# A two-layer transformer trunk on one core: norm total behind the row products, a norm root applied after the product, a rearranged end, and parked gates moved to the later head pairs

## The chip, the cores and the metric

The kernel runs on one core of one Trainium2 chip, in one launch. Its time is the device time in microseconds of that core. The kernel before took 2211.37 us, the median of three runs (2207.99 to 2211.55).

TensorE multiplies a stationary 128x128 block (the weight load, PEld) by a moving block of up to 512 columns and adds into PSUM; VectorE (DVE) and ScalarE (ACT) do elementwise work; SyncE (SP) issues most DMAs; ScalarE can issue DMAs too.

## The reference

Two layers work on 256 context and 256 latent tokens of 1024 channels (`SEQ = CTX_LEN = 256`, `D_MODEL = 1024`, `D_FF = 2816`), in float32. The output is the latent stream after a last norm.

```python
def rmsnorm(x, g):
    y = xf * lax.rsqrt(jnp.mean(xf * xf, axis=-1, keepdims=True) + EPS)
    return y * g
def modulate(h, shift, scale):
    return h * (1.0 + scale) + shift
def swiglu(h, wg, wu, wd):
    return (jax.nn.silu(h @ wg) * (h @ wu)) @ wd
def ffn_half(h_stream, m, gain, w):
    h = modulate(rmsnorm(h_stream, gain), m[0], m[1])
    return h_stream + 0.5 * m[2] * swiglu(h, *w)
...
# trunk_layer, latent stream (context likewise, but not in the last layer)
    x = ffn_half(x, ml[0:3], g[0], p['ffn1'])
    h = modulate(rmsnorm(x, g[1]), ml[3], ml[4])
    u, gq, gk, gv, nq, nk, nv, gates = split_in(h @ p['w_in'])
    y_ssm = s5_mixer(...); y_gqa = window_gqa_latent(...); y_na = neighborhood_attn_latent(...)
    m = sigmoid(g_s) * (y_ssm @ w_p_ssm) + sigmoid(g_a) * (y_gqa @ w_p_gqa) + sigmoid(g_n) * (y_na @ w_p_na)
    x = x + ml[5] * (m @ w_out)
    x = ffn_half(x, ml[6:9], g[2], p['ffn2'])
...
    return rmsnorm(x, final_g)
```

The modulations `ml`, `mc` are `silu(c) @ w_ada + b_ada`, nine of 1024 channels for each layer and stream.

## The kernel before

**Layout.** Channels lie on partitions: `X`, `Hh` and `Hl` are 128 x 8 x 512, columns 0 to 255 the context and 256 to 511 the latent tokens (`HALF` = 256). Every large product is done with both factors split into a high and a low part of a faster type, three matmuls for one (`mm3`, L83 to L85). A weight block of 128x1024 comes by DMA on SP (`wload`, L75), ScalarE makes its high part `whi` (L77), VectorE the remainder `wlo` (L79); three blocks are in flight. Product banks come from a pool of three in PSUM. A framework puts the instructions of each engine into one fixed order when the kernel is built, by priority in the order of the code and by its own model of times; `tc.issue_after(ins)` sets the instructions in its block that run on the engine of `ins` behind it.

**Norm.** `norm_sum` squares the eight blocks on ScalarE (L108) and adds them on VectorE (L109). `norm_total` sums over the partitions by a product with ones (L115, result `nps`). `norm_rsqrt` takes the reciprocal root in eleven small VectorE steps (L122 to L133). `norm_spread` makes it a block of 128 equal rows by products with the identity (L139, `nR`). `norm_apply` multiplies, shifts and splits each block into `Hh` and `Hl` (L158 to L160).

**Start** (`ffn_start`, from L266). The first layer's scale and shift come from row blocks of `w_ada` (`ada_rows`, L284): `products` (L305), `row_copy` (L311), transposition by `shift_scale` (L318, tile `pmod`), then three small VectorE operations (L193, L196). On TensorE `in_turn` keeps the order of the code: 18 warm-up products (`keep_warm`, L336), products of blocks 0 and 1, shift and scale, 12 warm-up products, norm total, spread, and then chunks of the first two feed forward steps between further row products. The two first weight blocks wait with their remainders behind the norm's root. DMAs on SP: row blocks 0 and 1, `X`, two weight blocks, row blocks 2 and 3, two weight blocks, and the rest.

**Mixer** (`mixer`). For each of four head pairs: queries of the windowed attention, its attention, keys, values and queries of the neighbourhood attention, its attention (`attend`: scores L821, softmax, transposition, values). The state-space part (`pump`) runs in pieces between. `gate(j)` is a projection of 24 matmuls and a tanh; `fill()` in front of each of the eight attentions computes gates ahead and parks them in DRAM, one each in layer 0 (seven in all, so none in front of the last), two each in layer 1 (eleven, so none in front of the last two). Three more gates stay on the chip, each behind one of the last three scores. After the attentions their memory is released; then come the splits of their results, the gated unit (`linear_unit`, tile `pgl`), the merge (`branch`, tile `pbr`) and the output product (tile `pwo`, L165 adds to `X`).

**Last feed forward** (`ffn` with one stream, layer 1, n = 1). Two weight blocks are loaded, the norm runs, and then both units of step 0 run block by block (`up`, `gate_up`), followed by steps 1 to 21 and two rounds of down products (tile `pd`). Only the 256 latent columns are computed.

**End** (L1167 to L1171). Norm sum, total, root and spread, then eight output operations, each with a DMA, over four buffers.

## Time and profile before

| what | before |
|---|---|
| median of the timed runs | 2211.37 us (2207.99 to 2211.55) |
| the profiled execution | 2205.09 us, its span 2203.3 us |
| TensorE matmul, busy | 2146.9 us, 97% |
| weight load | 1838.6 us, 83% |
| VectorE | 1621.1 us, 74% |
| ScalarE | 922.6 us, 42% |
| granted TensorE clock, mean | 0.98 |
| DMA | 368.64 MB, mean 167 GB/s |

The span is what the hardware profiler saw from the first to the last instruction of one execution. A busy matmul is not one at the peak: matmuls are pipelined and their ends are modelled, so distances between starts say more than durations. The granted clock is 1.00 at 2.4 GHz and 0.50 at 1.2 GHz. The idle time of an engine that isn't the bound costs nothing.

### The profile page before, as it was taken

To read this page: it belongs to the slowest core of one execution; us is meant where nothing else is said; L and a number is where in the kernel's file an instruction comes from. 1 tells how busy PE (TensorE), PEld (TensorE's weight loads), DVE (VectorE), ACT (ScalarE), POOL (GpSimd) and SP (SyncE) were. 2 spreads that over 40 slices of the span, in tenths; PEclk is the share of its full clock that TensorE was granted. 3 is DMA by queue.
4 is the path that set the end of the run, shared out by engine and by line. 5 is a ranking of instruction groups with operands and counts; after the bars stand their busy time and mean duration, and the time that the engine had idled before them with its cause. 6 is when DMAs were issued, how large, how long until landed. Compare 5 with 4: busy or idle time off the path is not lost. (4 is left out here: it accounts for less than half of the span.)

```text
span 2203.3 us, 32637 instructions
## 1 busy us (share of the span) xinstructions
PE 2146.9 (97%) x12354; PEld 1838.6 (83%) x12354; DVE 1621.1 (74%) x3164; ACT 922.6 (42%) x1560; POOL 0.7 (0%) x6
## 2 busy tenths in 40 slices
PE   7999999999998999999999999999999999999997
PEld 5888888977776888988888888888888888898997
DVE  4897887767765987886777698787857866665555
ACT  3322333466666323422222343223236755644443
POOL 0000000000000000000000000000000000000000
PEclk8999999999999999999999999999999999899999
DMA  8535544543432664675655455555546453453554
GB/s 315 175 119 175 197 159 148 192 134 115 149 106 70 214 221 148 203 231 158 199 198 163 133 165 188 168 170 180 172 125 207 157 172 101 153 198 125 173 191 124
DMA packets 134996, 368.64 MB, mean 167 GB/s; under 512 B 30132, under 2 KB 37044, under 8 KB 134840
## 3 DMA queue, kind: packets, MB, share of 16 engines
q1 hardware_dynamic: 134256, 366.44, 51.2%
q8 instruction: 97, 1.59, 0.3%
q14 instruction: 59, 0.48, 0.1%
q10 hardware_dynamic: 584, 0.12, 0.0%
HBM read 337.40 MB, written 29.11 MB: 166 GB/s over the span
## 5 line engine op out<-in xcount | busy, mean ns | idle before, releaser
L77 ACT ACTIVATE whi<-raw 128x1024 fp32r<-128x1024 f32 (+2 forms) x480 | 455.6, 950 | 950.7 <-issue 318.3
L79 DVE TENSOR_TENSOR wlo<-raw,whi 128x1024 fp32r<-128x1024 f32 (+2 forms) x480 | 520.8, 1087 | 275.0 <-ACT whi L77 273.1
L83 PE MATMUL pgu<-Hh,whi 128*128 128x512 f32 (+1 forms) x1360 | 494.4, 365 | 4.1 <-ACT Hh L159 2.7
L84 PE MATMUL pgu<-Hl,whi 128*128 128x512 f32 (+1 forms) x1360 | 494.3, 364 | 0.0
L85 PE MATMUL pgu<-Hh,wlo 128*128 128x512 f32 (+1 forms) x1360 | 493.8, 363 | 0.5 <-DVE wlo L79 0.5
L83 PEld LDWEIGHTS pgu<-Hh,whi 128*128 128x128 f32 x1360 | 257.9, 190 | 45.5 <-ACT Hh L159 4.4
L85 PEld LDWEIGHTS pgu<-Hh,wlo 128*128 128x128 f32 x1360 | 258.5, 190 | 40.7 <-DVE wlo L79 0.9
L84 PEld LDWEIGHTS pgu<-Hl,whi 128*128 128x128 f32 x1360 | 258.6, 190 | 39.7 <-DVE Hl L160 0.6
L83 PE MATMUL pd<-mid,whi 128*128 128x256 f32 (+1 forms) x836 | 281.1, 336 | 0.0
L84 PE MATMUL pd<-mid,whi 128*128 128x256 f32 (+1 forms) x836 | 280.5, 336 | 0.0
L85 PE MATMUL pd<-mid,wlo 128*128 128x256 f32 (+1 forms) x836 | 280.4, 335 | 0.0
L178 DVE SCALAR_TENSOR_TENSOR ajunk<-araw,sb 128x1024 f32<-128x1024 f32 x208 | 256.0, 1231 | 2.7
L83 PE MATMUL pp<-Hh,whi 128*128 128x512 f32 (+1 forms) x672 | 241.5, 359 | 0.8 <-ACT th L969 0.8
L85 PE MATMUL pp<-Hh,wlo 128*128 128x512 f32 (+1 forms) x672 | 240.4, 358 | 0.0
L84 PE MATMUL pp<-Hl,whi 128*128 128x512 f32 (+1 forms) x672 | 240.4, 358 | 0.0
L84 PEld LDWEIGHTS pd<-mid,whi 128*128 128x128 f32 x836 | 157.4, 188 | 17.8
L83 PEld LDWEIGHTS pd<-mid,whi 128*128 128x128 f32 x836 | 157.4, 188 | 17.8
L85 PEld LDWEIGHTS pd<-mid,wlo 128*128 128x128 f32 x836 | 157.3, 188 | 17.8
L83 PEld LDWEIGHTS pp<-Hh,whi 128*128 128x128 f32 x672 | 130.1, 194 | 17.4 <-ACT th L969 1.9
L84 PEld LDWEIGHTS pp<-Hl,whi 128*128 128x128 f32 x672 | 129.9, 193 | 17.1 <-issue 2.3
L85 PEld LDWEIGHTS pp<-Hh,wlo 128*128 128x128 f32 x672 | 129.7, 193 | 15.4 <-DVE wlo L79 0.2
L243 DVE TENSOR_TENSOR gact<-gact,pgu 128x512 f32<-128x512 f32 (+1 forms) x86 | 53.2, 618 | 70.9 <-PE pgu L85 70.6
(295 smaller groups left out, 2866.9 us busy)
## 6 DMA issues: line engine op xcount, KB each, us to landing
raw<-up SPq DMA_DIRECT2D x176, 512.0 KB, 3.9
araw<-ada SPq DMA_DIRECT2D x104, 512.0 KB, 4.1
raw<-win SPq DMA_DIRECT2D x90, 512.0 KB, 3.8
raw<-dn SPq DMA_DIRECT2D x76, 384.0 KB, 3.1
raw<-dn SPq DMA_DIRECT2D x76, 320.0 KB, 3.0
rw<-ada SPq DMA_DIRECT2D x24, 512.0 KB, 4.3
raw<-wout SPq DMA_DIRECT2D x24, 512.0 KB, 4.3
mid<-ada SPq DMA_DIRECT2D x32, 256.0 KB, 5.0
```

Of the source, the lines that this page charges most:

```text
L77: S.activation(hi[:, :n], raw[:, :n], AF.Copy)
L79: anchor[0] = V.tensor_sub(lo[:, :n], raw[:, :n], hi[:, :n].bitcast(F32)).ins
L83: PE.matmul(out, wh, ah, start=first, stop=False)
L84: PE.matmul(out, wh, al, start=False, stop=False)
L85: pe_anchor[0] = PE.matmul(out, wl, ah, start=False, stop=last).ins
L178: V.scalar_tensor_tensor(junk, raw, 1.0, sb[:, s], op0=ALU.mult, op1=ALU.mult, accum_out=mod[:, l, j, s:s + 1])
L243: V.tensor_mul(g[:, :N], g[:, :N], pu[:, :N])
```

## The change

It has four parts.

1. Start: the second row block's DMAs go to ScalarE's queue, the two tables `bada` and `ng` to SP behind `X`. On TensorE: 18 warm-up products, product of block 0, 9 warm-up products, product of block 1, norm total, shift and scale, spread. In all norms, the shift and the subtraction of the root's first guess become one step.
2. Mixer: the slots of `fill()` are 0, 1, 1, 1, 1, 1, 1, 1 in layer 0 and 1, 1, 1, 1, 1, 2, 2, 2 in layer 1. The three gates that stay may start behind the last query projection, behind the ninth-last score and behind the last score.
3. Last feed forward: `scaled` writes `X` times its coefficient, without the root, right behind each output block, and `shift_column` puts the shift into two columns ahead of the latent ones; the products take 258 columns. `gate_up_late` multiplies the product by the root and adds the shift's product. The norm's total runs between the two units of step 0, its spread behind them, in a PSUM bank of its own.
4. End: the last square goes into the total by its own products, without an addition; 4 and 9 idle products stand around the total; ScalarE scales `X` by the gain ahead of the root; three multiplications and DMAs of 3, 3 and 2 blocks write the output.

```diff
-        yi = y.bitcast(I32)
-        V.tensor_scalar(yi, x.bitcast(I32), 1, None, op0=ALU.arith_shift_right)
-        V.tensor_scalar(yi, yi, -1, 0x5F3759DF, op0=ALU.mult, op1=ALU.add)
+        V.tensor_scalar(y.bitcast(I32), x.bitcast(I32), -0.5, 0x5F3759DF, op0=ALU.mult, op1=ALU.add)
...
+    def norm_total_late(s):
+        cs = stream(s)
+        acc = npool.tile([128, HALF], F32, name="nacc", tag="nacc")
+        S.activation(acc, X[:, 0, cs], AF.Square)
+        for k in range(1, KC):
+            sq = npool.tile([128, HALF], F32, name="nsq", tag="nsq")
+            S.activation(sq, X[:, k, cs], AF.Square)
+            if k < KC - 1:
+                V.tensor_add(acc, acc, sq)
+        ps = nbank[0]("nps")
+        for x in (acc, sq):
+            for j in range(2):
+                pe_anchor[0] = PE.matmul(ps[:, j:j + 1], x[:, 128 * j:128 * j + 128], ones, start=x is acc and j == 0,
+                                         stop=x is sq, skip_group_check=True).ins
+        return ps[:, :2]
...
+    def scaled(l, i, k):
+        ca = coef[:, l, i, 0, k, 1:2]
+        S.activation(Hh[:, k, HALF:], X[:, k, HALF:], AF.Identity, scale=ca)
+        V.scalar_tensor_tensor(Hl[:, k, HALF:], X[:, k, HALF:], ca, Hh[:, k, HALF:].bitcast(F32), op0=ALU.mult, op1=ALU.subtract)
+
+    def shift_column(l, i):
+        cs = slice(HALF - 2, HALF)
+        cb = mod[:, l, 24 * i:24 * i + KC, 1:2].to_broadcast([128, KC, 2])
+        S.activation(Hh[:, :, cs], cb, AF.Copy)
+        V.tensor_sub(Hl[:, :, cs], cb, Hh[:, :, cs].bitcast(F32))
...
+    def gate_up_late(tp, mid, pg, pu, root):
+        late = tp.tile([128, 2], F32, name="late", tag="late", bufs=2)
+        g = tp.tile([128, T], F32, name="gact", tag="gact", bufs=2)
+        for j, p in enumerate((pg, pu)):
+            S.copy(late[:, j:j + 1], p[:, 0:1])
+            V.tensor_mul(g[:, HALF * j:HALF * j + HALF], p[:, 2:HALF + 2], root)
+        S.activation(g[:, :HALF], g[:, :HALF], AF.Silu, bias=late[:, 0:1])
+        V.scalar_tensor_tensor(g[:, :HALF], g[:, HALF:], late[:, 1:2], g[:, :HALF], op0=ALU.add, op1=ALU.mult)
+        split(mid[0][:, HALF:], mid[1][:, HALF:], g[:, :HALF])
...
-            blocks = [ada_rows(0), ada_rows(1)]
+            blocks = [ada_rows(0), ada_rows(1, nc.scalar)]
             for k in range(0, KC, 2):
                 nc.sync.dma_start(X[:, k:k + 2], A["xT"][:, k:k + 2])
+            for t, n in ((bada, "bada"), (ng, "ng")):
+                nc.sync.dma_start(t, A[n])
             in_turn(keep_warm, 18)
-            rows = row_copy(in_turn(products, blocks[0:2]))
-            in_turn(shift_scale, 0, rows)
-            in_turn(keep_warm, 12)
+            pr = in_turn(products, blocks[0:1])
+            in_turn(keep_warm, 9)
+            in_turn(products, blocks[1:2], pr, 1)
...
+            rows = row_copy(pr)
             ps = in_turn(norm_total, acc)
             y = norm_rsqrt(ps)
+            in_turn(shift_scale, 0, rows)
...
-                units = [(bank("pgu"), wload(A["up"][l, n, 0, j], 1024)) for j in range(2)]
-                pieces = norm(l, i, 1)
-                next(pieces)
-                with tc.issue_after(sums[0]), tc.issue_after(sums[1]):
-                    early.append(wload(A["up"][l, n, 1, 0], 1024))
-                for _ in pieces:
-                    pass
-                for k in range(KC):
-                    for ps, w in units:
-                        mm_k(ps[:, :HALF], w, k, HALF, T)
-                up(0, *(ps for ps, w in units))
+                acc = norm_sum(1)
+                first = unit(0, 0)
+                with tc.issue_after(pe_anchor[0]):
+                    y = norm_rsqrt(norm_total(acc))
+                second = unit(0, 1)
+                with tc.issue_after(pe_anchor[0]):
+                    spread = norm_spread(y)[:, :HALF]
+                root.append(tp.tile([128, HALF], F32, name="root", tag="root", bufs=1))
+                S.copy(root[0], spread)
+                up(0, first, second)
...
+        slots = [1, 1, 1, 1, 1, 2, 2, 2] if last else [0, 1, 1, 1, 1, 1, 1, 1]
 
         def fill():
-            for j in queue[:2 if last else 1]:
-                queue.remove(j)
+            for _ in range(slots.pop(0)):
+                j = queue.pop(0)
                 nc.sync.dma_start(parked[j, :, :N], gate(j)[:, :N])
...
             Q = na_queries(c)
+            last_query = pe_anchor[0]
             fill()
...
-        for j, behind in ((1, scored[-3]), (2, scored[-2]), (0, scored[-1])):
+        for j, behind in ((1, last_query), (2, scored[-9]), (0, scored[-1])):
...
-        R = norm_spread(norm_rsqrt(norm_total(norm_sum(1))))[:, :HALF]
+        idle(4)
+        with tc.issue_after(pe_anchor[0]):
+            ps = norm_total_late(1)
+        y = norm_rsqrt(ps)
         for k in range(KC):
-            o = tp.tile([128, HALF], F32, name="o", tag="o", bufs=4)
-            V.scalar_tensor_tensor(o, X[:, k, HALF:], fg[:, k:k + 1], R, op0=ALU.mult, op1=ALU.mult)
-            nc.sync.dma_start(A["out"][:, k], o)
+            S.activation(xg[:, k], X[:, k, HALF:], AF.Copy, scale=fg[:, k:k + 1])
+        idle(9)
+        with tc.issue_after(pe_anchor[0]):
+            R = norm_spread(y)[:, :HALF]
+        for a, b in ((0, 3), (3, 6), (6, 8)):
+            V.tensor_mul(o[:, a:b], xg[:, a:b], R.unsqueeze(1).to_broadcast([128, b - a, HALF]))
+            nc.sync.dma_start(A["out"][:, a:b], o[:, a:b])
```

## Rows read from the trace of the kernel before

**Rows 1.** The page's first part: engine, busy us, share of the span, instructions.
```profile
PE 2146.9 (97%) x12354; PEld 1838.6 (83%) x12354; DVE 1621.1 (74%) x3164; ACT 922.6 (42%) x1560; POOL 0.7 (0%) x6
```

**Rows 2.** Stretches (us), product tile `pgu` alone: length, TensorE busy (matmuls), clock, DMA.
```profile
80.00:120.00 40.00, 40.00 (x178) 1.00 0.51 164
2012.00:2052.00 40.00, 40.00 (x336) 1.00 0.60 196
```

**Rows 3.** Timeline of the start: start us, length us, engine, line, operation, [idle before].
```profile
13.94 5.48 DVE L350 TENSOR_TENSOR mid<-mid 128x512 f32<-128x512 f32 x7 [12.75 <-ACT mid L348]
...
18.21 1.86 PE L318 MATMUL pmod<-pick,rows 128*128 128x2 f32 x8 [6.07 <-ACT rows L311]
...
20.49 4.70 PE L336 MATMUL idle<-ident 128*128 128x128 f32 x24 [0.41 <-DVE mod L193]
...
25.04 0.95 PE L115 MATMUL nps<-ones,mid 128*128 128x1 f32 x8
...
26.22 0.17 DVE L124 TENSOR_SCALAR nt<-nt 128x4 int32<-128x4 int32 x1
...
28.09 2.36 DVE L79 TENSOR_TENSOR wlo<-raw,whi 128x1024 fp32r<-128x1024 f32 x2
...
31.84 1.22 PE L83 MATMUL pgu<-Hh,whi 128*128 128x512 f32 x2 [1.54 <-ACT Hh L159]
```

**Rows 4.** Stretches: length, PE, PEld, DVE, ACT, POOL busy (count), clock, DMA share, GB/s.
```profile
0.00:5.00 5.00, 3.65 (x17) 3.65 (x18) 0.35 (x3) 1.11 (x1) 0.70 (x6) 1.00 0.56 182
...
14.10:24.20 10.10, 5.57 (x25) 5.51 (x26) 5.08 (x10) 7.59 (x11) 0.00 (x0) 0.50 1.04 408
24.30:27.60 3.30, 1.69 (x16) 1.60 (x15) 1.31 (x8) 0.00 (x0) 0.00 (x0) 1.00 1.00 381
27.70:37.80 10.10, 8.04 (x28) 5.87 (x32) 8.19 (x15) 3.71 (x6) 0.00 (x0) 0.50 0.81 288
```

**Rows 5.** Stretches around the last attention of layer 0.
```profile
680.70:693.20 12.50, 6.91 (x20) 4.16 (x18) 7.22 (x18) 9.63 (x18) 0.00 (x0) 0.59 0.12 35
693.30:703.60 10.30, 10.25 (x63) 6.84 (x63) 5.27 (x14) 5.64 (x14) 0.00 (x0) 1.00 0.01 2
703.60:716.40 12.80, 12.80 (x57) 10.59 (x58) 10.21 (x14) 10.58 (x18) 0.00 (x0) 1.00 0.62 221
```

**Rows 6.** Timeline of TensorE there: the first scores.
```profile
683.93 0.80 PE L821 MATMUL sc<-K,Q 128*128 128x256 f32 x2 [2.90 <-DVE Q L753]
```

**Rows 7.** Stretches up to and around the last attention of layer 1.
```profile
1780.00:1870.00 90.00, 88.58 (x568) 74.43 (x568) 67.25 (x146) 56.03 (x116) 0.00 (x0) 0.95 0.46 146
...
1879.00:1886.50 7.50, 3.82 (x8) 1.91 (x8) 5.52 (x12) 5.89 (x13) 0.00 (x0) 0.50 0.33 62
1886.50:1891.20 4.70, 4.70 (x23) 4.69 (x22) 3.07 (x8) 4.31 (x8) 0.00 (x0) 0.50 0.00 0
1891.40:1905.90 14.50, 13.34 (x107) 11.70 (x105) 6.66 (x14) 8.57 (x19) 0.00 (x0) 1.00 0.44 147
```

**Rows 8.** Timeline of TensorE: the last product of the output projection.
```profile
1991.25 0.28 PE L85 MATMUL pwo<-mgh,wlo 128*128 128x256 f32 x1
```

**Rows 9.** Stretches of the last feed forward: its first step, then steady steps.
```profile
1998.20:2004.00 5.80, 5.75 (x26) 5.61 (x27) 5.46 (x14) 3.01 (x7) 0.00 (x0) 0.50 0.23 79
2004.00:2006.60 2.60, 2.60 (x24) 2.60 (x24) 0.00 (x0) 0.04 (x1) 0.00 (x0) 1.00 0.00 0
2010.00:2040.00 30.00, 30.00 (x252) 30.00 (x252) 17.09 (x23) 14.55 (x22) 0.00 (x0) 1.00 0.62 201
```

**Rows 10.** Timeline of the end.
```profile
2191.56 0.43 DVE L109 TENSOR_TENSOR nacc<-nacc,nsq 128x256 f32<-128x256 f32 x1 [0.54 <-ACT nsq L108]
...
2194.88 1.03 PE L139 MATMUL nR<-ident,nt 128*128 128x128 f32 x4 [2.23 <-DVE nt L133]
...
2198.43 1.96 DVE L1170 SCALAR_TENSOR_TENSOR o<-X,fg,nR 128x256 f32<-128x256 f32 x4 [0.83 <-DMA out_dram<-o]
```

**Rows 11.** DMA issues of the last 14 us: operation, count, size, us to landing.
```profile
out_dram<-o SPq DMA_DIRECT2D x8, 128.0 KB, 2.0
```

More of the change, by code (lines that the diff above doesn't have):

```diff
@@ L275, in ffn_start @@
             nc.scalar.dma_start(pick, A["pick"])
-            for t, n in ((bada, "bada"), (ng, "ng")):
-                nc.scalar.dma_start(t, A[n])
             sT = st.tile([128, KC, 32], F32, name="sT")
@@ L280, in ffn_start, with ada_rows, hidden @@
             S.activation(sT[:, :, :2], cT, AF.Silu)
-            def ada_rows(k):
+            def ada_rows(k, queue=nc.sync):
                 w = [mid_tile(tp, i % 2).bitcast(F32).rearrange("p (q c) -> p q c", q=2) for i in range(4)]
                 for i in range(4):
-                    nc.sync.dma_start(w[i], A["ada0"][k, :, 2 * i:2 * i + 2])
+                    queue.dma_start(w[i], A["ada0"][k, :, 2 * i:2 * i + 2])
                 return w
-            def hidden(f):
-                for j in range(2):
+            def hidden(f, *js):
+                for j in js:
                     w = wload(A["up"][0, 0, f, j], 1024, st, f"{f}{j}")
@@ L298, in in_turn, with products @@
                 return r
-            def products(blocks):
-                pr = bank("prow")
-                for i, w in enumerate(blocks):
+            def products(blocks, pr=None, first=0):
+                pr = bank("prow") if pr is None else pr
+                for i, w in enumerate(blocks, first):
                     for h in range(2):
@@ L350, in ffn_start @@
                     V.tensor_add(acc, acc, sq)
+            rows = row_copy(pr)
             ps = in_turn(norm_total, acc)
             y = norm_rsqrt(ps)
+            in_turn(shift_scale, 0, rows)
             with tc.issue_after(sums[1]):
-                hidden(0)
+                hidden(0, 0)
+                hidden(0, 1)
             blocks += [ada_rows(2), ada_rows(3)]
             with tc.issue_after(sums[1]):
-                hidden(1)
+                hidden(1, 0, 1)
             blocks += [ada_rows(k) for k in range(4, KC)]
@@ L391, in ffn @@
         c0 = HALF * streams[0]
-        early = []
+        h0 = c0 if both else c0 - 2
+        root = []
         def unit(f, j):
-            w, ps = early.pop() if early else wload(A["up"][l, n, f, j], 1024), bank("pgu")
+            w, ps = wload(A["up"][l, n, f, j], 1024), bank("pgu")
             for k in range(KC):
-                mm_k(ps[:, :T - c0], w, k, c0, T)
+                mm_k(ps[:, :T - h0], w, k, h0, T)
             hook(0.01 * (T - c0))
@@ L403, in up @@
             pg, pu = [*done, *(unit(f, j) for j in range(len(done), 2))]
-            gate_up(tp, mids[f], pg, pu, c0, T)
+            if both:
+                gate_up(tp, mids[f], pg, pu, c0, T)
+            else:
+                gate_up_late(tp, mids[f], pg, pu, root[0])
         def down(half, a, b, ms=range(KC), between=None):
@@ L1106, in mixer @@
                 evac_x(m, ps, l, 1, a, b)
+                if last:
+                    scaled(l, 2, m)
+        if last:
+            shift_column(l, 2)
         norms_in(None, None)
@@ L1163, in body, with idle @@
             else:
-                ffn(tp, l, 1, (1,), lambda us: None)
-    with tc.tile_pool(name="fin", bufs=1) as tp:
-        R = norm_spread(norm_rsqrt(norm_total(norm_sum(1))))[:, :HALF]
-        for k in range(KC):
-            o = tp.tile([128, HALF], F32, name="o", tag="o", bufs=4)
-            V.scalar_tensor_tensor(o, X[:, k, HALF:], fg[:, k:k + 1], R, op0=ALU.mult, op1=ALU.mult)
-            nc.sync.dma_start(A["out"][:, k], o)
+                with tc.tile_pool(name="rp", bufs=1, space=PSUM) as rp:
+                    norms_in(rp, "norm")
+                    ffn(tp, l, 1, (1,), lambda us: None)
+                    norms_in(None, None)
+    with tc.tile_pool(name="fin", bufs=1) as tp, tc.tile_pool(name="finp", bufs=1, space=PSUM) as fp:
+        xg = tp.tile([128, KC, HALF], F32, name="xg")
+        o = tp.tile([128, KC, HALF], F32, name="o")
+        def idle(n):
+            w = fp.tile([128, 128], F32, name="idle", tag="idle")
+            with tc.issue_after(pe_anchor[0]):
+                for _ in range(n):
+                    pe_anchor[0] = PE.matmul(w, ident, ident, start=True, stop=True).ins
+        idle(4)
+        with tc.issue_after(pe_anchor[0]):
+            ps = norm_total_late(1)
+        y = norm_rsqrt(ps)
+        for k in range(KC):
+            S.activation(xg[:, k], X[:, k, HALF:], AF.Copy, scale=fg[:, k:k + 1])
+        idle(9)
+        with tc.issue_after(pe_anchor[0]):
+            R = norm_spread(y)[:, :HALF]
+        for a, b in ((0, 3), (3, 6), (6, 8)):
+            V.tensor_mul(o[:, a:b], xg[:, a:b], R.unsqueeze(1).to_broadcast([128, b - a, HALF]))
+            nc.sync.dma_start(A["out"][:, a:b], o[:, a:b])
     es.close()
```

## The prediction

> **What bounds the kernel now.** I read the page's busy times first: TensorE is busy in 97% of the span [rows 1], so nearly every microsecond to be won is one in which TensorE waits or runs at its lower clock. Then I looked for these places: distances of over 0.8 us between the starts of two matmuls in the timeline. They sit in four clusters, and the change touches each: the first 32 us; the end of the last neighbourhood attention in either layer's mixer; the first step of the last feed forward; and everything behind the last matmul. Between them the pace is steady: 178 matmuls of 512 columns in 40 us, 0.225 us each, and 336 of 256 columns, 0.119 us each [rows 2]. A full gate (24 matmuls) is thus 5.4 us in layer 0 and 2.86 us in layer 1.
>
> **Start.** The sum of squares is complete when the last addition ends, 13.94 + 5.48 = 19.42, but the norm total starts at 25.04 [rows 3]. What stands between is TensorE's own order: the row transposition waits 6.07 us for the row copy, which ScalarE does behind the squares, and then twelve warm-up products (24 passes, 4.70 us) are in the queue. The change puts the total straight behind the second row product, so it can start at 19.4: minus 5.6. One VectorE step of the reciprocal root goes (0.17 us, 0.2 with its gap): minus 0.2. Against this, the total now falls into the stretch where the granted clock is 0.50, from 14.1 to 24.2 [rows 4], where eight passes take about 1.8 us, as the row transposition's eight do, instead of 0.95: plus 0.85. The transposition now runs beside the root chain; its three small VectorE operations come ahead of the two weight remainders (2.36 us) that the first normalised chunk already waits behind: plus 0.6, less what the spread hid, so nothing to plus 0.8. The first product moves from 31.84 to about 27, some 5 us.
>
> What that is worth depends on the clock. Now it is 1.2 GHz from 14.1, 2.4 GHz from 24.3 to 27.6 once the warm-up products had run, and 1.2 GHz again to 37.8 after TensorE had stood idle around the spread [rows 4]. If it is again 1.2 GHz to 37.8, the 5 us are worked at half rate and bring 2.5. If it stays at 2.4 GHz, the first chunk also loses its half rate: 6 us at half, 3 us more, 8 in all. The idle stretch ahead of the first chunk is still there, so I take **4 us**, bounds 2.5 and 8. Row block 1 goes to ScalarE's DMA queue, so four issues stand less ahead of X on SP; in the first 5 us the DMA engines are at 0.56, and at 1.04 between 14.1 and 24.2 [rows 4]. I take nothing for it: X arrives in the saturated stretch, and the seven additions behind its squares keep their own pace (5.48 us). The two small tables that go to SP stand behind X and are needed only by the three small operations. (The Trainium skill, "DMA: Bandwidth & Descriptors", section "Issuing engines are not separate DMA queues", says that issuing from several engines saves issue time only. If the idle 0.44 of the first 5 us were all issue time, X would land 2.2 us sooner and this term would be 6; the sum does without it.)
>
> **Parked gates.** Layer 0 has seven parked gates for eight head-pair attentions and now leaves the first without one, no longer the last; layer 1 has eleven, two each for the first five, and now 1, 1, 1, 1, 1, 2, 2, 2. Each costs a weight load, its two splits, a tanh and a DMA write on SP: the same number as before, moved. On SP a write waits for its tanh; behind the moved ones stand the loads for the gated unit and the merge, which start over 20 us later. Two of the three gates kept on chip may also start earlier: behind the last query projection and behind an earlier score.
> Layer 0: from 680.7 to 693.2 TensorE is busy 6.91 of 12.5 us at a granted 0.59, then nearly full [rows 5]; the first score alone waits 2.90 us for the queries [rows 6]. At full clock the busy time up to 716.4 is some 28 us (6.91 at 0.59 lies between 4.1 and 6.9, taken as 5; 10.25; 12.8). With one gate more it is 33.4, and it starts 5.4 earlier, because the first attention's stretch has key, value and query projections to fill it. Without a wait the merge would start at 680.7 - 5.4 + 33.4 = 708.7 instead of 716.4: 7.7. If the softmax chain, not TensorE, sets the end, only the 5.4 remain; and two gates ahead of the first score would lengthen that chain by 10.8 less the 2.9 it waits anyway, so 2.5 would be lost. I take **6**, near the first, because TensorE is full again from 693.3; bounds -2.5 and 7.7.
> Layer 1: 1879 to 1886.5 is busy 3.82 of 7.5 at 0.50, then 4.70 at 0.50, then 13.34 of 14.5 at full clock [rows 7]; at full clock about 17.8. Two gates more make 23.5, begun 5.7 earlier: 1879 - 5.7 + 23.5 = 1896.8 instead of 1905.9, 9.1. By the chain alone it is 5.7, less the 2 by which two gates outlast the 3.7 idle us: 3.7; with four gates ahead of the scores 2 are lost. I take **4.5**, bounds -2 and 9.1. The weights of the merge can't load before the attention's memory is released, which bounds both from above. The five attentions that lose a gate keep one; their stretch is 98% busy now (88.58 of 90 us [rows 7]), and later projections can move in, so I count that at zero. If that cover fails, see the third rival.
>
> **First step of the last feed forward.** From the last output product at 1991.25 [rows 8] to the end of the first 48 up products there pass 15.4 us: 50 recorded in 1998.2 to 2004 at 0.50 and on to 2006.6 at 1.00, two of them counted in both windows [rows 9]. Now the columns are scaled beside the output products, the root is applied to the product, and the norm lies between two units. That is 48 products by 0.12, the total (0.5) and the spread (0.8, both with the switch of kind): 7.1 us. Minus 8.3. The last column block's update, scaling and split (three operations of 256 columns; the addition of that size took 0.43 [rows 10]) are hidden by its unit's first seven blocks, 21 by 0.12 = 2.5 us. The products become 258 columns wide: (0.225 - 0.119)/256 is 0.41 ns a column, 1056 products by 0.83 ns is plus 0.9. (The Trainium skill, "TensorE: Matmul & The Clock Gate", section "Back-to-back issue gap", gives sustained spacings from which a column is 0.13 ns, an estimate, and this 0.3 us; the windows speak against it, and the sum goes by them.) Each step gets about 1 us more of VectorE work (two multiplications of 256 columns and a wider last one) and 0.4 of ScalarE. VectorE is busy 17.09 of 30 us there [rows 9]; with 1.0 more per 5.7 us it is 75%, so TensorE hides it. I take **7.2**; if a bank comes free late at the seams of the two halves, 5.
>
> **End.** One addition (0.43 and its gap [rows 10]) and one root step go: 0.65. The spread took 1.03 us in four passes; at full clock, kept by the idle products, 0.65: 0.4. The output is then one multiplication over up to 768 columns three times instead of eight operations, the last four of which wait for buffers and end at 2200.39 [rows 10]; with a landing of 2.0 [rows 11] that is 6.5 behind the spread. By the 1.18 us of a 1024-column remainder [rows 3] the three take 0.9, 0.9 and 0.6; with the landing and 0.7 for the larger pieces 5.1: 1.4 sooner. Against it: nine idle products are 18 passes; at 0.11 us they end as the root does (2.0 us), at half clock they hold the spread up by 1.6. I take **2.2**, bounds 0.5 and 2.5.
>
> **Sum.** 4 + 6 + 4.5 + 7.2 + 2.2 = 23.9. The profiled execution took 2205.09 (span 2203.3, 1.8 around it) and would take 2181.2. It lies 6.3 under the median of the timed runs, 2211.37; the same 23.9 from the median gives **2187.5**. The one removed root step in the other norms is hidden under other work.
>
> **Rivals.**
> Gates where they were: the scheduler places an instruction by its own model, and a bound that is looser need not be used; or the chain of the last attention ends last anyway. Then the two middle terms are gone: 13.4, so **2198**. For it: the last attention's first score waits for its own queries, which no gate shortens. Against: 5.6 us of idle time in 12.5.
> All at the upper bounds: 8 + 7.7 + 9.1 + 7.4 + 2.5 = 34.7, so **2177**. It needs the clock to hold in all stretches.
> Starved attentions, the slower side: six attentions have one gate less (one in layer 0, five in layer 1). Where one starves, TensorE idles for the lost cover, at least 2.9 us, and falls to 1.2 GHz for a stretch like the 10.1 us of [rows 4], which costs 5 more: 7.9 each. From four on, the loss exceeds the 23.9; all six are 47 us, so **2235**. Against it: 98% busy with two gates, and 16.5 us of projections per pair (two of 5.4, two of 2.86) to pull forward. With two of them starved and no gain at the tails (13.4 - 15.8), the time is unchanged, about **2214**.
>
> **How the numbers follow.** My forecast 0.52, its own range 2180 to 2195; gates without effect 0.20; all at the upper bound 0.14; unchanged 0.08; slower 0.06. Range 2175 to 2202: from just under the upper case to the case without gates with the start at its lower bound and the seams late (2198 + 1.5 + 2.2). A difference under 0.2% (4.4 us) can't be told from none here. Faster: 0.52 + 0.20 + 0.14 = 0.86; same 0.08; slower 0.06.
>
> **What would show it.** In the changed profile: the norm total at 19 to 20 us and the first chunk near 27; gate products between the last queries and the first scores of both layers, with the granted clock at 1.00 through layer 0's last attention; no gap over 1 us between the output products and the second up unit, and a pace of 0.120; the spread at the end within 4.5 us of the last product. The forecast is wrong if scores in the earlier attentions wait over 1 us with no products between, if the first chunk still runs at 0.50 to the end, or if TensorE waits for root multiplications in the last feed forward.

## The result and the profile after

The changed kernel took **2179.59 us** (median, 2176.96 to 2180.91) beside 2209.68 us (2204.75 to 2211.55) for the kernel before: ratio 0.9866, 95% interval 0.9845 to 0.9886, 30.1 us faster. The forecast was 23.9 us, 2187.5 us, with a range from 2175 to 2202; the time lies in this range, but 0.4 us below the forecast's own 2180 to 2195. The profiled execution took 2176.96 us, its span is 2175.2, 28.1 less than before's.

The first part of the page of the changed kernel stands against [rows 1]: engine, busy us, share, instructions.

```profile
PE 2135.0 (98%) x12378; PEld 1829.7 (84%) x12378; DVE 1630.7 (75%) x3184; ACT 931.6 (43%) x1614; POOL 0.7 (0%) x6
```

**Where the time went.** I cut every trace at the same marks, each the start of a matmul: the first down product of the first feed forward, the last product of tile `pbs` ahead of a mixer's head pairs, the first and the last output product (`pwo`), the last down product (`pd`). The column "without" is the mean over the profiled executions that don't have the part (before and the one-part kernels below), "with" the mean over those that have it unaltered; in brackets the lowest and highest.

| stretch, us | before | after | without | with | forecast |
|---|---|---|---|---|---|
| start to first `pd` | 165.35 | 161.49 | 165.2 (164.2-166.3) | 161.2 (159.8-162.2) | -4 |
| layer 0, last `pbs` to first `pwo` | 416.02 | 408.94 | 416.2 (416.0-416.5) | 409.0 (408.9-409.1) | -6 |
| layer 1, last `pbs` to first `pwo` | 286.97 | 279.57 | 288.6 (287.0-289.4) | 278.4 (277.9-279.6) | -4.5 |
| last `pwo` to last `pd` | 198.96 | 190.52 | 198.4 (198.1-199.0) | 190.4 (190.2-190.7) | -7.2 |
| last `pd` to the end | 13.05 | 11.07 | 13.1 (13.05-13.24) | 11.1 (11.07-11.30) | -2.2 |

The gains of the means are 4.0, 7.2, 10.2, 8.0 and 2.0, in sum 31.4. The stretches between them took 0.7 to 6.4 us more in the executions of the changed kernel and its variants than in that of before, and most of it goes with TensorE's clock: from layer 0's first output product to layer 1's mark it is 821.3 us in the execution (the changed kernel's) without a stretch at 1.2 GHz there, 823.1 to 823.6 in the five that have 3.4 us of it, and 825.1 to 826.7 in the three that have 6.8 or 10.2. What makes the clock fall in one execution and not in another isn't shown. So the total came out 6 us better than forecast, and nearly all of that is layer 1's mixer.

**Start**, timeline of the changed kernel, against [rows 3]: start us, length us, engine, line, operation, [idle before <- what ended it].

```profile
2.60 5.30 SPq L376 DMA_DIRECT2D X<-xT  x4
...
8.84 1.15 ACT L386 ACTIVATE mid<-X 128x512 f32<-128x512 f32 x2 [3.32 <-DMA X<-xT]
...
11.52 0.33 SPq L378 DMA_DIRECT2D bada<-bada  x1
...
13.44 1.43 SPq L75 DMA_DIRECT2D raw<-up  x2
...
16.41 1.05 PE L115 MATMUL nps<-ones,mid 128*128 128x1 f32 x8 [0.61 <-DVE mid L388]
...
20.37 1.06 ACT L77 ACTIVATE whi<-raw 128x1024 fp32r<-128x1024 f32 x1 [2.39 <-DMA raw<-up]
21.33 0.57 ACT L347 COPY rows<-prow 128x512 f32<-128x512 f32 x1
...
21.95 1.87 PE L354 MATMUL pmod<-pick,rows 128*128 128x2 f32 x8 [4.49 <-ACT rows L347]
...
23.86 0.16 DVE L221 TENSOR_TENSOR mod<-pmod,bada 128x4 f32<-128x4 f32 x1 [5.20 <-PE pmod L354]
...
24.74 2.08 PE L154 MATMUL nR<-ident,nt 128*128 128x128 f32 x8 [0.92 <-DVE nt L131]
...
28.35 1.22 PE L83 MATMUL pgu<-Hh,whi 128*128 128x512 f32 x2 [1.53 <-ACT Hh L174]
```

The norm total starts 8.6 us sooner than before, 3 sooner than I said, and yet the first product comes only 3.5 sooner. Read from the bottom up: the spread waits for the root, the root on VectorE stands behind a modulation step (L221) that waits 5.20 us for `pmod`, `pmod` waits 4.49 us for the row copy, and the copy stands on ScalarE behind a weight split that waits 2.39 us for its DMA. The products of the copy's rows had long been done. One operation without its data holds up three engines, only because it is ahead in the order.

In the kernel before, the two weight blocks are issued from 9.38 us on, and both splits (19.02 and 19.97) find their data. Timeline of before:

```profile
6.11 2.54 SPq L340 DMA_DIRECT2D X<-xT  x4
...
9.38 1.73 SPq L75 DMA_DIRECT2D raw<-up  x2
...
12.76 4.93 ACT L348 ACTIVATE mid<-X 128x512 f32<-128x512 f32 x8 [7.36 <-DMA X<-xT]
```

In the changed kernel they are issued from 13.44 us on, behind the two tables; ScalarE is ready for the second split 2 us sooner than before, but its data is there only at 20.37, later than before. The view of SyncE's waits (who waits for what, us in total, times, longest; SPq is its queue of DMA issues) says why they are issued late:

```profile
SPq L378 <- DMA mid<-ada: 3.6, 1, 3.6
SPq L75 <- DMA mid<-ada: 1.9, 2, 1.1
```

The first table waits 3.6 us for the DMA of a row block (tile `mid`), a wait that the kernel before doesn't have; the weight blocks behind it wait another 1.9, much as before (1.8). No run here puts the tables elsewhere, so how much of the start that alone would bring isn't shown.

The windows of the same stretch (length, PE, PEld, DVE, ACT, POOL busy (count), clock, DMA share, GB/s) show that the clock is 1.2 GHz for 13.6 us around this pause, in one stretch instead of the two of 10.1 in [rows 4], and that the DMA engines are full. The first chunk, twelve products from 28.35 to 33.6, still runs at 0.50 to its end:

```profile
20.00:33.60 13.60, 9.19 (x28) 7.32 (x28) 8.57 (x19) 6.19 (x9) 0.00 (x0) 0.50 1.01 370
33.60:40.00 6.40, 6.40 (x65) 4.58 (x68) 0.44 (x4) 0.58 (x1) 0.00 (x0) 1.00 0.99 338
```

**Last attentions**, windows of the changed kernel, the first three of layer 0 against [rows 5], the last three of layer 1 against [rows 7]:

```profile
668.00:681.00 13.00, 13.00 (x60) 10.78 (x60) 4.08 (x6) 7.39 (x9) 0.00 (x0) 1.00 0.21 56
681.00:692.00 11.00, 10.99 (x60) 7.80 (x58) 8.77 (x25) 8.57 (x24) 0.00 (x0) 1.00 0.13 43
692.00:706.20 14.20, 13.34 (x69) 9.68 (x67) 9.05 (x15) 11.23 (x21) 0.00 (x0) 1.00 0.52 186
...
1850.00:1860.00 10.00, 10.00 (x77) 8.86 (x74) 2.96 (x5) 2.81 (x6) 0.00 (x0) 0.99 0.32 107
1860.00:1866.00 6.00, 6.00 (x39) 6.00 (x40) 0.57 (x1) 2.11 (x6) 0.00 (x0) 0.73 0.28 44
1866.00:1890.00 24.00, 23.17 (x178) 20.70 (x177) 18.19 (x39) 20.64 (x42) 0.00 (x0) 1.00 0.39 129
```

TensorE has hardly a gap left: it is busy 37.33 of 38.2 us in layer 0 and 39.17 of 40 in layer 1, where before 6.91 of 12.5 and 3.82 of 7.5 were busy in the worst stretches. Its clock stays at 2.4 GHz in layer 0; in layer 1 a short stretch at 1.2 GHz is left where 17.1 us were before.

**First step of the last feed forward**, timeline of TensorE in the changed kernel, against [rows 8]; between these rows stand the 48 up products, and the third unit begins at 1980.63:

```profile
1973.59 0.28 PE L85 MATMUL pwo<-mgh,wlo 128*128 128x256 f32 x1
1976.56 0.50 PE L115 MATMUL nps<-ones,nacc 128*128 128x1 f32 x4
1980.20 0.68 PE L154 MATMUL nR<-ident,nt 128*128 128x128 f32 x4 [0.17 <-DVE nt L131]
```

Windows of that step and of later ones in the changed kernel, against [rows 9]:

```profile
1973.70:1980.60 6.90, 6.73 (x57) 6.55 (x56) 4.18 (x15) 2.58 (x5) 0.00 (x0) 1.00 0.27 83
2010.00:2040.00 30.00, 30.00 (x255) 30.00 (x253) 20.30 (x32) 14.87 (x33) 0.00 (x0) 1.00 0.53 166
```

TensorE is busy 6.73 of 6.90 us in the first step. VectorE is busy 20.30 of 30 us in the later ones (17.09 before), and TensorE stays full.

**End**, timeline of the changed kernel, against [rows 10, 11]. Last product 2164.11, spread 4.22 us behind it, then the three multiplications:

```profile
2164.11 0.28 PE L85 MATMUL pd<-mid,wlo 128*128 128x256 f32 x1
2164.23 1.05 PE L1227 MATMUL idle<-ident 128*128 128x128 f32 x8
...
2166.16 2.25 PE L1227 MATMUL idle<-ident 128*128 128x128 f32 x18
...
2168.33 0.71 PE L154 MATMUL nR<-ident,nt 128*128 128x128 f32 x4
2169.15 2.42 DVE L1239 TENSOR_TENSOR o<-xg,nR 128x768 f32<-128x768 f32 x3 [0.87 <-PE nR L154]
```

### The profile page after: what moved, and what is told of

The parts are those of the page before. It is cut to its first block, busy times and chain, and to the rows that moved or that the text cites. A ratio compares the mean times of both kernels' runs of the same rounds, so it can differ in the third digit from the quotient of the medians.

```text
span 2175.2 us, 32666 instructions
## 1 busy us (share of the span) xinstructions
PE 2135.0 (98%) x12378; PEld 1829.7 (84%) x12378; DVE 1630.7 (75%) x3184; ACT 931.6 (43%) x1614; POOL 0.7 (0%) x6
## 5 line engine op out<-in xcount | busy, mean ns | idle before, releaser
L85 PEld LDWEIGHTS pd<-mid,wlo 128*128 128x128 f32 x836 | 157.2, 188 | 19.4 <-DVE wlo L79 1.4
L271 DVE TENSOR_TENSOR gact<-gact,pgu 128x512 f32<-128x512 f32 x64 | 43.8, 684 | 54.4 <-PE pgu L85 54.1
```

The costliest lines, as they stand in the source:

```text
L85: pe_anchor[0] = PE.matmul(out, wl, ah, start=False, stop=last).ins
L271: V.tensor_mul(g[:, :N], g[:, :N], pu[:, :N])
```

## The experiments

### Each part alone

Each kernel is the kernel before with one part of the change (the root keeps its eleven steps). The lines that mark each, all from the change:

```diff
# e1_start
+            blocks = [ada_rows(0), ada_rows(1, nc.scalar)]
...
+            rows = row_copy(pr)
             ps = in_turn(norm_total, acc)
# e2_gates
+        slots = [1, 1, 1, 1, 1, 2, 2, 2] if last else [0, 1, 1, 1, 1, 1, 1, 1]
...
+        for j, behind in ((1, last_query), (2, scored[-9]), (0, scored[-1])):
# e3_ffn
+        h0 = c0 if both else c0 - 2
...
+                gate_up_late(tp, mids[f], pg, pu, root[0])
# e4_end
+        idle(4)
...
+        for a, b in ((0, 3), (3, 6), (6, 8)):
```

> The kernel before with the start alone changed (DMA queues, warm-up products, norm total ahead of shift and scale; the root keeps its eleven steps). Theory of separate parts: the changed kernel's trace gains 3.5 us up to the first chunk (28.35 against 31.84), and the start alone should do the same: first product at 28 to 29, the start of the first down product 3.5 to 4 us sooner, span 2199 to 2200, time about 2206 against a median of 2209.7. Rival, a gain that is worked off again: the later stretches are bound by VectorE's filler work or by DMA, and the end comes less than 1 us sooner.

> The kernel before with the parked gates alone changed (slots, and the bounds of the three gates that stay on the chip). Theory of separate parts: layer 0's merge starts 6 to 7 us sooner and layer 1's another 6 to 8, together 13 to 14 us, span about 2190, time about 2196. Rival: part of what the changed kernel shows in the mixers comes from the shorter start, by another place of the granted clock's stretches; then this run gains under 9 us.

> The kernel before with the last feed forward alone changed (scaled columns, root behind the product, 258 columns, own bank for the norm). Theory of separate parts: 8.3 to 8.7 us between the last output product and the last down product, none of it given back by 258 columns, span about 2194.7, time about 2201. Rival: the 258 columns cost 0.9 us in 1056 products, as the pace of 512 and 256 columns suggests, and the gain is 7.4.

> The kernel before with the end alone changed (last square without an addition, idle products, gain ahead of the root, three output pieces; the root keeps eleven steps). Theory: 1.8 us, that is the 2.0 of the changed kernel less the root step; span about 2201.5, time about 2208. Rival: the end hides behind the DMA landing, under 0.7 us.

Measured beside 2207.31 us for the kernel before:

| kernel | median, us | difference | ratio, 95% interval |
|---|---|---|---|
| e1_start | 2205.67 | -1.6 | 0.9993, 0.9983 to 1.0002 |
| e2_gates | 2193.24 | -14.1 | 0.9937, 0.9918 to 0.9956 |
| e3_ffn | 2198.75 | -8.6 | 0.9967, 0.9951 to 0.9983 |
| e4_end | 2205.38 | -1.9 | 0.9990, 0.9980 to 1.0000 |

The differences add to 26.2 us; the whole change is 27.7 under the same median (30.1 beside its own runs). So the parts hardly touch one another, and the gates are worth over half. The start's time can't be told from none by its interval, and the end's interval reaches 1.0000. The start's own stretch is 3.2 us shorter in the trace than before's, yet the profiled execution ends 0.6 us later (span 2203.9): 1.4 us are lost again ahead of the mixer, where it has a stretch at 1.2 GHz that before's execution doesn't have, 0.9 between the mixers and 1.9 in layer 1's mixer, where before's was the shortest of four. So the start's gain is shown for its stretch, not at the end of the kernel, and the expectation's rival isn't excluded. The other three came out near their theories, the gates with 10.6 us in layer 1 against the mean (9.0 against before's trace), more than the 6 to 8 expected.

### Which part of the gates: the moved ones or the looser bounds

In the changed kernel, g1 puts back the three bounds, g2 the slots, and g3 pushes the parked gates further back.

```diff
# g1_slots
-        for j, behind in ((1, last_query), (2, scored[-9]), (0, scored[-1])):
+        for j, behind in ((1, scored[-3]), (2, scored[-2]), (0, scored[-1])):
# g2_bounds
-        slots = [1, 1, 1, 1, 1, 2, 2, 2] if last else [0, 1, 1, 1, 1, 1, 1, 1]
+        slots = [2, 2, 2, 2, 2, 1, 0, 0] if last else [1, 1, 1, 1, 1, 1, 1, 0]
# g3_late
-        slots = [1, 1, 1, 1, 1, 2, 2, 2] if last else [0, 1, 1, 1, 1, 1, 1, 1]
+        slots = [0, 0, 0, 0, 0, 3, 4, 4] if last else [0, 0, 0, 0, 1, 2, 2, 2]
```

> The changed kernel with the bounds of the three gates that stay on the chip put back (behind the third-last, second-last and last score); the new slots of the parked gates stay. Between the last queries and the first scores of the last attention one parked gate is left in layer 0 (two stood there) and two in layer 1 (three). Measured against the changed kernel by its landmarks: in layer 0 the merge starts at 706.33 us there, in layer 1 at 1889.75 us. Theory (the parked gate moved to the last attentions fills the wait for the queries by itself, 5.4 us of work against a wait of 2.9; the looser bounds add only what is left): merge at most 1.5 us later in layer 0 and at most 2.5 us later in layer 1, clock 1.00 in layer 0's last attention. Rival (the gain comes from a gate that may start behind the last query, that is from the bounds): merge 3.5 us or more later in layer 0 and 4 or more in layer 1, with an idle stretch of over 1.5 us inside the last attention.

> The changed kernel with the slots of the parked gates as in the kernel before (2, 2, 2, 2, 2, 1, 0, 0 and 1 in each of the first seven); the looser bounds of the three gates that stay on the chip remain. Theory (the gates moved bring the gain: 5.4 us of work out of a stretch that is full anyway into one that waits): with the bounds alone the merge starts 4 to 6 us later than in the changed kernel in layer 0 and 5 to 8 later in layer 1, which leaves a gain of 1 to 3 us in each over the kernel before, by the wait for the queries that the kept gate covers. Rival (the bounds are what counts): merge at most 2 us later than in the changed kernel in both layers.

> The changed kernel with the parked gates pushed further back: slots 0, 0, 0, 0, 1, 2, 2, 2 in layer 0 and 0, 0, 0, 0, 0, 3, 4, 4 in layer 1, so that four and five attentions have none. Theory (an attention without a gate is filled by projections pulled forward, which is why the change lost nothing there): no stretch before the last head pair with over 2 us of idle time more than in the changed kernel, the last attention's first scores later by the gates now ahead of them (5.4 each in layer 0, 2.86 in layer 1) but the merge later by 0 to 4 us in each layer; time 0 to 6 us over the changed kernel's. Rival (starved attentions): each attention that has no gate loses at least 2.9 us of cover, and 7.9 where the clock falls: seven of them 20 to 55 us slower than the changed kernel, with scores that wait for their queries or keys with no products between.

| us | no part of it | slots alone (g1) | bounds alone (g2) | both | pushed further (g3) |
|---|---|---|---|---|---|
| layer 0, last `pbs` to first `pwo` | 416.2 | 413.0 | 409.7 | 409.0 | 405.6 |
| layer 1, last `pbs` to first `pwo` | 288.6 | 283.7 | 285.3 | 278.4 | 281.0 |
| time (g1 to g3: one execution) | | 2187.77 | 2187.07 | 2179.59 | 2177.87 |

I take the first output product as the mark, because in g1 gates of layer 1 still stand behind the first merge product. (By the expectations' own mark, the first merge product counted from the last `pbs`, g1 is 4.3 us later than the changed kernel in layer 0, and g2 2.4 in layer 0 and 5.7 in layer 1.) My theory, that the moved gates bring the gain, falls in layer 0: the bounds alone bring 6.5 of 7.2 us, the slots alone 3.2. In layer 1 it takes both: 4.9 and 3.3 alone, 10.2 together. Two waits of TensorE show why. Timeline of TensorE in the last attention of layer 0, g1:

```profile
681.81 0.84 PE L865 MATMUL sc<-K,Q 128*128 128x256 f32 x3 [2.86 <-ACT pr L833]
```

and of layer 1, g2:

```profile
1885.33 0.80 PE L865 MATMUL sc<-K,Q 128*128 128x512 f32 x2 [3.08 <-ACT pr L833]
```

Both are scores that wait for the softmax of earlier ones (tile `pr`, ScalarE), not for the queries. In g1, layer 1, it is more:

```profile
1880.39 0.50 PE L865 MATMUL sc<-K,Q 128*128 128x512 f32 x1 [4.03 <-ACT pr L833]
```

In the kernel before, this wait shows less, because there the scores wait for the queries. Timeline of before, layer 0, behind the 2.90 us of [rows 6]:

```profile
686.57 0.79 PE L821 MATMUL sc<-K,Q 128*128 128x256 f32 x2 [1.85 <-DVE Q L753]
687.73 1.40 PE L821 MATMUL sc<-K,Q 128*128 128x256 f32 x3 [0.36 <-ACT pr L789]
```

Covering the first wait uncovers the second. A parked gate stands ahead of the attention and covers the wait for the queries; a kept gate, bound behind the last query alone, is cut into pieces by the order and fills the pauses between scores: in the changed kernel 13 of its products stand behind the first scores of layer 0, and one to five in each later pause. These are two different waits, and the prediction gave the looser bounds no price of their own. In g2, layer 1, no parked gate is left for the front, so the kept one is used up there and is missing behind.

g3 speaks on the starved attentions. Windows of g3, layers 0 and 1, ahead of the last attention:

```profile
443.00:662.00 219.00, 217.05 (x1240) 167.81 (x1239) 158.64 (x403) 145.90 (x346) 0.00 (x0) 1.00 0.36 121
...
1681.00:1850.00 169.00, 162.37 (x1017) 138.55 (x1016) 124.44 (x275) 109.19 (x225) 0.00 (x0) 0.93 0.44 139
```

and the same stretches in the changed kernel:

```profile
443.00:662.00 219.00, 214.39 (x1200) 164.67 (x1198) 158.98 (x404) 146.61 (x344) 0.00 (x0) 1.00 0.37 121
1681.00:1850.00 169.00, 163.32 (x1047) 139.66 (x1048) 126.27 (x275) 111.59 (x228) 0.00 (x0) 0.95 0.45 144
```

Nine attentions without a gate (one in the changed kernel) cost none of the 20 to 55 us: in layer 0 the idle time there even falls from 4.6 to 2.0 us, since projections are pulled forward (1240 products in the same window instead of 1200), and the layer gains 3.4 us more. In layer 1 it rises from 5.7 to 6.6 us, the clock is lower (0.93 instead of 0.95), and the layer loses 2.6 against the mean. My expectation missed the sign of layer 0.

### The start: order on ScalarE, or the DMA queue

x1 puts the row copy ahead of the weight splits and the modulation steps behind the root.

```diff
...
             y = norm_rsqrt(ps)
-            in_turn(shift_scale, 0, rows)
             with tc.issue_after(sums[1]):
+                in_turn(shift_scale, 0, rows)
+            with tc.issue_after(sums[1]), tc.issue_after(copied[0]):
                 hidden(0, 0)
...
```

> The changed kernel with an order at the start: ScalarE's row copy ahead of the splits of the first two weight blocks and of the modulation rows, and the shift and scale's VectorE operations behind the root. Theory: the changed kernel's norm total ended at 17.5, but its first product came at 28.35 because on ScalarE the copy stands behind a weight split that waits 2.39 us for its DMA, and on VectorE an operation that waits for the copy's result stands in the middle of the root (5.20 us). With the order given, the root is done by 19.6 and the first product comes when the second block's remainder is there, at 22 to 23.5; the first down product comes 4 to 6 us sooner than in the changed kernel, time 2174 to 2176. Rival: the stretch is bound by DMA (share 0.9 to 1.0 up to 30 us), so the chunks wait for weights and row blocks instead and the first down product comes less than 1.5 us sooner.

Measured 2180.77 us (ratio 0.9884, 0.9864 to 0.9903): no gain; the first down product comes at 161.12 us instead of 161.49, as the rival had it. Timeline of x1:

```profile
17.86 1.03 PE L354 MATMUL pmod<-pick,rows 128*128 128x2 f32 x8
...
20.04 2.08 PE L154 MATMUL nR<-ident,nt 128*128 128x128 f32 x8 [1.15 <-DVE nt L131]
...
27.71 1.06 ACT L77 ACTIVATE whi<-raw 128x1024 fp32r<-128x1024 f32 x1 [3.35 <-DMA raw<-up]
28.67 0.90 ACT L174 ACTIVATE Hh<-nh,mod 128x256 fp32r<-128x256 f32 x2
...
29.21 1.22 PE L83 MATMUL pgu<-Hh,whi 128*128 128x512 f32 x2 [7.09 <-ACT Hh L174]
```

The waits I named are gone and the spread starts 4.7 us sooner. But then a third weight split without its DMA stands on ScalarE ahead of the second normalised block, and the first product comes at 29.21 instead of 28.35. The wait was moved, not removed: again a split without its DMA stands ahead of an operation that is urgent.

So the next kernel changes when the DMAs go out: the second row block goes to SyncE, behind `X`, and nothing of it to ScalarE's queue.

```diff
-            blocks = [ada_rows(0), ada_rows(1, nc.scalar)]
+            blocks = [ada_rows(0)]
             for k in range(0, KC, 2):
                 nc.sync.dma_start(X[:, k:k + 2], A["xT"][:, k:k + 2])
+            blocks.append(ada_rows(1))
```

> The changed kernel with the second row block on SP's queue behind X, instead of ScalarE's queue. Theory, the order of the transfers: the first square starts as early as in the changed kernel (8.84, within 0.7 us; 12.76 before), since X still stands ahead of block 1; the second block's products end up to 3 us later, still not after 18 us; the first product of the first chunk within 1 us of 28.35. Rival, the second queue: the first square comes at 10.5 or later.

> The changed kernel with all four DMAs of the second row block on SyncE's queue behind those of the input, none on ScalarE's, now timed in rounds (one look at the same kernel: first product at 25.86 us against 28.35, end of the span 2.3 us earlier). Theory (the row copy and the second weight split no longer stand in each other's way, since both have their data when ScalarE comes to them; the 2.5 us at the first product last to the end): ratio to the kernel before 0.985 to 0.9865, 1.5 to 3 us under the changed kernel beside the same runs. Rival (a start that is 2.5 us earlier meets the same weight blocks, and the one look is chance): within 1 us of the changed kernel's 2179.6.

One execution took 2174.65 us; over five the same kernel took **2172.98 us** (2172.44 to 2176.32) beside 2208.25, ratio 0.9844, 0.9831 to 0.9857. Timeline of b1_queue:

```profile
2.60 3.06 SPq L376 DMA_DIRECT2D X<-xT  x4
...
11.69 1.58 SPq L75 DMA_DIRECT2D raw<-up  x2
...
17.11 1.06 ACT L77 ACTIVATE whi<-raw 128x1024 fp32r<-128x1024 f32 x1 [1.06 <-DMA raw<-up]
18.07 0.57 ACT L347 COPY rows<-prow 128x512 f32<-128x512 f32 x1
...
18.53 1.06 ACT L77 ACTIVATE whi<-raw 128x1024 fp32r<-128x1024 f32 x1
...
21.34 2.07 PE L154 MATMUL nR<-ident,nt 128*128 128x128 f32 x8 [0.72 <-DVE nt L131]
...
24.95 1.22 PE L83 MATMUL pgu<-Hh,whi 128*128 128x512 f32 x2 [1.53 <-ACT Hh L174]
```

The weight blocks are issued 1.75 us sooner than in the changed kernel. The copy now stands between the two splits, the second split has its data, and the first product comes 3.4 us sooner (25.86, 2.5 sooner, in the first execution, where the expectation said within 1 us). The stretch to the first `pd` is 157.1 and 158.7 us, 3.3 under the mean of 161.2. The time is below the changed kernel's by 6.6 us; but the changed kernel didn't run beside it and their two ratios' intervals just overlap, so I take the 3.3 of the stretch as shown and leave the rest open. The ratio lies just below the 0.985 to 0.9865 expected. This version beats the kernel before; that its whole time beats the changed kernel's isn't shown. On the first square the expectation left a space between its two cases: 10.05 us in the one execution, 9.04 in the other, 8.27 to 9.75 in the kernels with two queues.

### The width of 258, and the idle products

w1 makes the products 320 columns wide (62 more columns than needed, not used); n1 leaves out the idle products of the end.

```diff
# w1_320
...
-        h0 = c0 if both else c0 - 2
+        h0 = c0 if both else c0 - 64
# n1_no_idle
-        idle(4)
...
-        idle(9)
```

> The changed kernel with 320 columns instead of 258 in the last feed forward's up products (62 more that nothing uses). The changed kernel's up products run at 119.05 ns with 258 columns, the ones before at 120.0 with 256. Theory, columns set the pace: 0.41 ns a column as between 256 and 512, so 145 ns, and 1056 products make 27 us more. Rival, something else has set the pace up to about 260 columns and goes on to set it: 125 ns or less, under 7 us more.

> The changed kernel without the 4 and 9 idle products at the end. Theory: TensorE stands idle around the total, so the granted clock is at 0.50 when the spread runs, or falls a little later; the four passes take 0.4 us longer at most, and the span behind the last down product, 11.1 us in the changed kernel, is 11.0 to 11.6. Rival: the idle products matter for more than the spread, and it is over 12.

w1: the stretch from the last `pwo` to the last `pd` is 218.96 us, 28.5 over the changed kernel's 190.4; over 1056 products that is 27.0 ns for 62 columns, 0.44 ns a column. Windows of the up products alone, of the changed kernel and then of w1:

```profile
1990.00:2030.00 40.00, 40.00 (x338) 1.00 0.54 181
```

```profile
1990.00:2030.00 40.00, 40.00 (x275) 1.00 0.45 153
```

From 258 to 320 columns set the pace, with nearly the slope of the prediction (0.41). But at 258 columns 338 products fit in 40 us, and 336 at 256 [rows 2]; the 528 of the second half are 119.05 ns apart in the changed kernel and 119.99 before. The first two extra columns cost nothing that shows, while 0.83 ns a product, 0.9 us in all, had been worked out. Why they are free isn't settled.

n1: 11.59 us from the last product to the end instead of 11.07 (time 2178.07). Its timeline:

```profile
2166.25 0.61 PE L147 MATMUL nps<-ones,nsq 128*128 128x1 f32 x4 [0.96 <-ACT nsq L141]
2168.89 1.23 PE L154 MATMUL nR<-ident,nt 128*128 128x128 f32 x4 [2.03 <-DVE nt L131]
```

Without the idle products the spread runs at 1.2 GHz, 1.23 us instead of 0.71. That is the 0.5 us they bring.

## Why the prediction was right

The sign and the places were right, and the time lies in the range, but the sum of 23.9 was 6 low, nearly all by one term. The time lies nearer to the rival "all at the upper bounds" (2177) than to the forecast (2187.5). One of the signs that the prediction named for being wrong did appear: the first chunk still ran at 0.50 to its end.

**Start: 4, measured 4.0, by a wrong way.** The step that failed is "X arrives in the saturated stretch", taken as no gain from the moved row block: the first square came at 8.84 us, not 12.76, and the total at 16.4, not 19.4. Against it stood something that the prediction didn't list, ScalarE's order: it said that the transposition "now runs beside the root chain", and it ran in the middle of it, 5.20 us late. It also passed over the tables as "needed only by the three small operations", and didn't ask what stands behind them on SyncE: the two weight blocks, issued 4.1 us later than before. That these misses cancel to the 4 of the sum is luck. As to the Trainium skill, "DMA: Bandwidth & Descriptors", section "Issuing engines are not separate DMA queues": it says that several issuing engines share the same DMA engines and save issue time only. The runs agree: with two queues the eight issues of `X` and the second row block are out at 7.9 us in the changed kernel, with one at 9.4 (b1_queue), but the first product is sooner with one. What brought `X` forward is its place ahead of the second row block on SyncE, which both have: its issues start at 2.60 us instead of 6.11.

**Layer 0's gates: 6, measured 7.2**, within the bound of 7.7, but only in part for its reason: it priced the moved gate ahead of the scores, and g2 has 6.5 of it without that gate. The rows of before showed the wait for the queries; the wait for the softmax that the kept gate fills shows in full only once the first is covered. **Layer 1's gates: 4.5, measured 10.2** (7.4 between the two profiled executions), past the bound of 9.1. This is the term that was mis-sized. "By the chain alone" I let the softmax set the end and charged two gates 2 us for outlasting an idle stretch; in fact a kept gate fills the pauses between scores, and with the pauses goes the stretch at 1.2 GHz (17.1 us before, 3.4 after). Also, the profiled execution of before had the shortest of four such stretches (286.97 against 288.9 to 289.4), so its rows understated the loss. "I count that at zero" for the attentions that lose a gate was nearly right: pauses of over 0.3 us ahead of the last pair add to 4.7 us in layer 1 instead of 2.1, none over 0.92; in layer 0 to 3.2 instead of 3.1, the longest 1.00 (1.48 before).

**Last feed forward: 7.2, measured 8.0** (8.4 between the profiles). The first step came out as worked out: 7.04 us from the last `pwo` to the third unit against 15.4. The 0.9 for the extra columns, which the runs show to cost nothing, was the error; the root multiplications are hidden, as said.

**End: 2.2, measured 2.0.** The spread took 0.7 us at full clock (0.65 forecast), the multiplications 2.42 (2.4). The larger pieces land in 2.5 us instead of 2.0.

**The rivals.** Gates without effect falls by e2: 14 us. Starved attentions falls by the changed kernel's time and by g3. All at the upper bounds gave 2177, 2.6 us from the measured time, but with another make-up: one term beyond its bound, the start far from its own, and the clock not held in the first chunk.

## What to carry to other kernels

Where an engine works in a fixed order, look for the operation that stands ahead of the urgent one and lacks its data; taking it away pays only if the next in line has its data, so ask first when each DMA lands, and what its issue waits for in its own queue. An attention whose softmax lasts longer than its products has two pauses, ahead of the scores and between them, and needs independent products allowed in both. Cut several traces at the same marks before a term is sized: a single trace had the loss here at 7.4 where the mean is 10.2.

## What the runs showed of the hardware

The product of 258 columns is no slower than that of 256 (338 against 336 in 40 us), although from 258 to 320 each column costs 0.44 ns. TensorE's short stretches at 1.2 GHz come at the same places of the program in all kernels (near 420, 1270, 1650, 1760 and 1820 us), but not each in every execution, and not equally long. From the first `pd` to the last `pbs` of layer 0, the two executions without the one near 420 took 278.0 and 278.1 us, the twelve with it 279.3 to 279.8. The four DMA issues of `X` took SyncE 3.72 to 5.80 us in the eight kernels in which ScalarE issued the second row block, and 2.54 to 3.71 in the six in which SyncE did; of the changed kernel's 5.30 the profile puts 3.5 down to waits for row blocks' DMAs.
